# Turning V and K by VectorE and a DRAM scratch in the token mixer of a decoder layer, in place of TensorE transposes

## The chip, the cores and the metric

The kernel is one program on one core of a Trainium2 chip. Its time is device microseconds of one execution. The engines have a queue of instructions each and work through it in order: TensorE (PE; PEld are its weight loads), VectorE (DVE), ScalarE (ACT), GpSimd (POOL), and SyncE (SP), which here issues nearly all DMA transfers. An instruction whose data are not there stops its engine, and with it everything that stands behind it.

## The reference

One layer of a hybrid decoder for 280 tokens: 16 meta tokens and 256 prompt tokens (a sequence), and 8 tokens of 8 running requests. Model width 2048, all data fp32. The layer is FFN, mixer, FFN, each with a residual and a layer norm. What matters here is the mixer: one input projection makes ten parts, from which two branches follow.

```python
q_r, k_r, v_r, g_r, q_h, f_h, i_h, g_h, a_r, a_h = jnp.split(x @ w_in, N_PROJ, axis=-1)
# retention, 8 heads of 256, per chunk
o = jnp.einsum('bhij,bhjv->bhiv', inner, v) + jnp.einsum('bhid,bhdv->bhiv', q_dec, S)
S_new = jnp.exp(lg * C)[:, None, None].astype(S.dtype) * S + jnp.einsum('bhjd,bhjv->bhdv', k_dec, v)
# HGRN2, 16 heads of 128, per chunk
S_new = jnp.exp(b_last[:, :, 0, :, None]) * S + jnp.einsum('bhjd,bhjv->bhdv', k_dec, v)
```

A projection leaves its result with features on partitions and tokens along the free axis. The state updates contract over tokens (`j`), so `k_dec` and `v` must have tokens on partitions there, and the outputs need `v` in the same form. So V and K have to be turned once per head.

## The kernel before

Every large product is three fp32r matmuls: weights and tokens are split into a rounded part and a residue, and high x high, low x high, high x low are summed. Weights come in loads of eight 128x128 blocks, in the order in which they are used: `load` fetches `raw` (512 KB, SP queue, three buffers), ScalarE rounds it to `whi` (L188, three buffers), VectorE subtracts for `wlo` (L189, three buffers). So a load of `raw` can leave once the `wlo` three loads earlier is made, and `whi` of a load can be made once TensorE has used up the load three earlier. One load is 24 matmuls.

The mixer projects in groups of two column chunks (four loads a group). There are eight passes `u`, each one retention head and two HGRN2 heads: `qkv_groups(u)` in the order f, q_h, i_h, q_r, k_r, v_r, and the gate groups of the pass before. `evacuate` takes each result out of PSUM. Beside the projection run generators: after i_h `mix_hg(u)` is started, after v_r `mix_ret(u)`. `pump` is called after every k step of the projection and lets a generator go on when its count (the numbers after `yield`) is down. That is how the mixers' instructions come to stand between the projection's matmuls. TensorE's order is exactly the order written (`manual_schedule`); the order on ScalarE, VectorE, GpSimd and SP is set by the framework's scheduler when the program is built, and is fixed then.

Names of the change: `v` is a value part of the projection, `vth` and `vtr` the turned values of HGRN2 and retention, `kth` the turned HGRN2 K (one per head, `turned(h)`), `ks` and `vs` the split K and V of retention, `pst` (L1022, L1024) the HGRN2 state update, `psr` (L1168) the retention state update, `po` and `por` the outputs. `smh` and `vbh` are the running requests' states and values of an HGRN2 head; their loads for the second head are opened by small GpSimd copies that read `kth` (L769, L773), so they leave after it exists. `turned`, in the change, is a scratch in DRAM.

Turning is done by TensorE: `nc.tensor.transpose` of a 128x128 block into PSUM (L875 for i_h, L982 for K, L1107 for v_r, L1114 for k_r), and a ScalarE copy of two blocks out of it (L879, L983, L1108; for k_r the scaled split of L1129 and L1130 reads PSUM itself). That is sixteen transposes a pass.

## Time and profile before

| | us |
|---|---|
| three runs: median (lowest to highest) | 2566.79 (2566.35 to 2567.9) |
| profiled execution: span | 2563.9 |
| profiled execution: its own time | not recorded beside the span |
| TensorE busy | 2553.4 |
| VectorE busy | 1702.8 |
| ScalarE busy | 1392.2 |
| GpSimd busy | 57.0 |
| mean DMA rate, GB/s | 209 |

The median of the runs lies 2.9 us above the span of the profiled execution. The mixer lies between 745 and 1690 us of the span. In the profile's lists a row names the source line, the engine, the operation, what is written and read, and either (groups) the count, the busy time in us, the mean duration in ns and the idle time before, or (timelines) the start and the duration in us, merged over neighbours of one kind. The duration of a matmul holds its way through the array, so two matmuls in a row overlap in it; what one costs in a stream is the distance of the starts.

### The profile page before, as it was taken

The numbers are of one execution on the slowest core, as the hardware profiler recorded it, in microseconds if no ns is written. First come the engines' busy times: TensorE is split into PE (matmuls) and PEld (weight loads), VectorE is DVE, ScalarE is ACT, GpSimd is POOL, SyncE is SP. The second block draws the span as 40 slices with busy tenths as digits, with TensorE's granted clock in tenths as the row PEclk, the third lists the DMA queues.
The fourth block names the chain that finished last, engine by engine and source line by source line (L and its number), as shares of the span: only waits on it lengthen the run. The fifth ranks groups of instructions, "written<-read, shape, count | busy, mean of one in ns | idle before, by whom it ended". The sixth has DMA issues, their size and how long they took to land.

```text
span 2563.9 us, 56275 instructions
## 1 busy us (share of the span) xinstructions
PE 2553.4 (100%) x23424; PEld 2534.4 (99%) x23424; DVE 1702.8 (66%) x2827; ACT 1392.2 (54%) x2186; POOL 57.0 (2%) x152
## 2 busy tenths in 40 slices
PE   9999999999999999999999999999999999999999
PEld 9999999999999999999999999999999999999998
DVE  6444544475569878777777777777885555556555
ACT  5444444444456767767676666675564444444443
POOL 0000000000000000000000000000000000000000
PEclk9999999999999999999999999999999999999999
DMA  7555555555555876767676767675556565565554
GB/s 244 183 187 183 187 182 184 186 182 186 184 201 180 287 265 232 264 214 260 212 264 215 259 223 255 224 239 188 196 190 197 194 197 195 194 196 195 195 195 149
DMA packets 156897, 536.26 MB, mean 209 GB/s; under 512 B 17952, under 2 KB 25952, under 8 KB 156640
## 3 DMA queue, kind: packets, MB, share of 16 engines
q1 hardware_dynamic: 156352, 532.37, 62.0%
q8 instruction: 183, 3.00, 0.5%
q14 instruction: 74, 0.61, 0.1%
q10 hardware_dynamic: 288, 0.29, 0.0%
HBM read 501.99 MB, written 30.61 MB: 208 GB/s over the span
## 4 chain that ended last, share of the span: by engine, by line
PE 96%; DVE 2%; ACT 0%; issue 0%; DMA 0%; SPq 0%; ACTq 0%; DVEq 0%
PE up L218 36%; PE dn L218 19%; PE pj_i_h L218 3%; PE pj_g_r L218 3%; PE pj_q_h L218 3%; PE pj_g_h L218 3%; PE pj_a_r L218 3%; PE pj_a_h L218 3%; PE pj_f L218 3%; PE pj_q_r L218 3%; PE pj_k_r L218 3%; PE wo L218 3%; PE pj_v_r L218 3%; DVE wlo L189 1%; PE pqr L1211 1%; PE psr L1168 0%
## 5 line engine op out<-in xcount | busy, mean ns | idle before, releaser
L189 DVE TENSOR_TENSOR wlo<-raw,whi 128x1024 fp32r<-128x1024 f32 (+1 forms) x869 | 1062.2, 1223 | 740.7 <-ACT whi L188 737.3
L188 ACT CAST whi<-raw 128x1024 fp32r<-128x1024 f32 (+1 forms) x870 | 905.7, 1042 | 909.2 <-PE up L218 411.0
L218 PE MATMUL up<-xh,whi 128*128 128x280 f32 (+1 forms) x2624 | 725.6, 280 | 0.6 <-ACT whi L188 0.6
L218 PE MATMUL up<-xh,wlo 128*128 128x280 f32 (+1 forms) x2624 | 725.8, 280 | 0.4 <-DVE wlo L189 0.3
L218 PE MATMUL up<-xl,whi 128*128 128x280 f32 (+1 forms) x2624 | 725.4, 279 | 0.0
L218 PEld LDWEIGHTS up<-xh,wlo 128*128 128x128 f32 x2624 | 492.6, 189 | 1.0 <-DVE wlo L189 1.0
L218 PEld LDWEIGHTS up<-xh,whi 128*128 128x128 f32 x2624 | 492.6, 189 | 0.8 <-ACT whi L188 0.8
L218 PEld LDWEIGHTS up<-xl,whi 128*128 128x128 f32 x2624 | 492.6, 189 | 0.0
L218 PE MATMUL dn<-hh,whi 128*128 128x280 f32 (+1 forms) x1376 | 384.7, 280 | 0.0
L218 PE MATMUL dn<-hh,wlo 128*128 128x280 f32 (+1 forms) x1376 | 384.3, 279 | 0.0
L218 PE MATMUL dn<-hl,whi 128*128 128x280 f32 (+1 forms) x1376 | 384.3, 279 | 0.0
L218 PEld LDWEIGHTS dn<-hh,whi 128*128 128x128 f32 x1376 | 260.1, 189 | 0.1
L218 PEld LDWEIGHTS dn<-hl,whi 128*128 128x128 f32 x1376 | 260.1, 189 | 0.1
L218 PEld LDWEIGHTS dn<-hh,wlo 128*128 128x128 f32 x1376 | 260.1, 189 | 0.0
L218 PE MATMUL pj_k_r<-xh,whi 128*128 128x280 f32 x256 | 74.2, 290 | 0.0
L218 PE MATMUL pj_g_r<-xh,whi 128*128 128x264 f32 x256 | 74.0, 289 | 0.0
L218 PE MATMUL pj_v_r<-xh,whi 128*128 128x280 f32 x256 | 73.8, 288 | 0.0
L218 PE MATMUL pj_v_r<-xh,wlo 128*128 128x280 f32 x256 | 72.4, 283 | 0.3 <-DVE wlo L189 0.3
L218 PE MATMUL pj_g_h<-xh,whi 128*128 128x264 f32 x256 | 72.7, 284 | 0.0
L218 PE MATMUL pj_k_r<-xh,wlo 128*128 128x280 f32 x256 | 72.4, 283 | 0.0
L218 PE MATMUL pj_v_r<-xl,whi 128*128 128x280 f32 x256 | 72.3, 283 | 0.0
L218 PE MATMUL pj_k_r<-xl,whi 128*128 128x280 f32 x256 | 72.3, 283 | 0.0
(421 smaller groups left out, 5263.4 us busy)
## 6 DMA issues: line engine op xcount, KB each, us to landing
raw<-in_w_up SPq DMA_DIRECT2D x343, 512.0 KB, 4.1
raw<-in_w_in SPq DMA_DIRECT2D x320, 512.0 KB, 4.3
raw<-in_w_dn SPq DMA_DIRECT2D x172, 512.0 KB, 3.5
smr<-in_sr SPq DMA_DIRECT2D x32, 512.0 KB, 5.0
out_srs<-smr SPq DMA_DIRECT2D x32, 512.0 KB, 6.7
raw<-in_w_out SPq DMA_DIRECT2D x32, 512.0 KB, 3.9
vbr<-vrd SPq DMA_DIRECT2D x32, 256.0 KB, 4.1
smh<-in_sg SPq DMA_DIRECT2D x16, 512.0 KB, 5.2
```

Of the source, the lines that this page charges most:

```text
L188: nc.scalar.copy(hi[:, j:jn, :], raw[:, j:jn, :])
L189: nc.vector.tensor_tensor(out=lo[:, j0:j1, :], in0=raw[:, j0:j1, :], in1=hi[:, j0:j1, :].bitcast(F32), op=ALU.subtract)
L218: nc.tensor.matmul(o, w, t, start=start, stop=stop)
L1211: nc.tensor.matmul(pq[32 * j : 32 * j + 32, :256], qdr_at[c][:, 32 * b : 32 * b + 32], sms[2 * e + c][:, j, :], start=e + c == 0, stop=e + ...
```

## The change

V of both branches, K of HGRN2 and K of retention are no longer turned by TensorE. VectorE transposes every 32x32 block of a 128x256 tile within itself (`nc.vector.transpose`, straight out of PSUM for the values), writing the blocks so that four DMA transfers put them at their mirrored places in a DRAM scratch and a fifth reads the whole tile back in rows (`turned_over`). That is five calls a pass (i_h, two K, k_r, v_r) and 25 transfers, all on SP. The turned tiles have the layout (token in block, feature, chunk, block), so TensorE and the other engines read them with a stride of two or four elements. `ks` and the values' split read the turned tiles from SBUF; `v` serves as the staging tile for three of the calls, `k` for K. The ends and tails of the tokens that do not fill a block of 128 are still transposed by TensorE; ScalarE copies them out of PSUM now, where GpSimd took them from `v`.

```diff
@@ evacuate
                 elif n == "i_h":
...
+                    ends = tmp("ends", (P, 2, 2, NMETA))
+                    vt = tmp("vth", TURNED)
+                    v = tmp("v", TURNED)
+                    for j, o in enumerate(st.pop("i_h", (o0, o1))):
+                        nc.vector.transpose(pieces(v, j), o[:, NMETA:LP])
+                        nc.scalar.copy(ends[:, j, 0, :], o[:, :NMETA])
+                        nc.scalar.copy(ends[:, j, 1, :], o[:, T - NMETA : T])
+                    turned_over(vt, v)
...
+                    if n == "k_r":
+                        st["ks"] = ks = tmp("ks", (P, 2, *TURNED[1:]), dt=F32R, bufs=4, tag="smr")
+                        z = tmp("v", TURNED)
+                        for j in range(2):
+                            nc.vector.transpose(pieces(z, j), r[:, j, : 2 * P])
+                        turned_over(ks[:, 1].bitcast(F32), z)
...
                 elif n == "v_r":
-                    v = tmp("v", (P, 2, T))
-                    nc.scalar.copy(v[:, 0, :], o0)
-                    nc.scalar.copy(v[:, 1, :], o1)
-                    start(mix_ret(c0 // 2, st["q_r"], st["k_r"], v), 24 if c0 == 2 else 3)
+                    vt = tmp("vtr", TURNED)
+                    v = tmp("v", TURNED)
+                    for j, o in enumerate((o0, o1)):
+                        nc.vector.transpose(pieces(v, j), o[:, : 2 * P])
+                        nc.scalar.copy(tails[:, 2 + j, : T - 2 * P], o[:, 2 * P :])
+                    turned_over(vt, v)
+                    start(mix_ret(c0 // 2, st["q_r"], st["k_r"], st["ks"], vt), 24 if c0 == 2 else 3)
...
+            TURNED = (P, P, 2, 2)
...
+            def pieces(z, c):
+
+                return z[:, :, c].rearrange("p (i f) b -> p b i f", i=4)
+
+            def turned_over(out, z):
+
+                n = math.prod(z.shape[1:]) // 4
+                y = drp.tile([4, 32, 4, n], F32, tag=f"turned{n}", name="turned")
+                for i in range(4):
+                    nc.sync.dma_start(
+                        y[:, :, i, :].rearrange("j t r -> t j r"),
+                        z[32 * i : 32 * i + 32].rearrange("t (j f) c b -> t j (f c b)", j=4))
+                nc.sync.dma_start(out.rearrange("t f c b -> t (f c b)"), y.rearrange("j t i r -> (j t) (i r)"))
...
@@ mix_hg
                 for h in range(2):
 
-                    pt = mx_bank("pt")
-                    for b in range(2):
-                        nc.tensor.transpose(pt[:, b * P : (b + 1) * P], v[:, h, NMETA + b * P : NMETA + (b + 1) * P], ident)
...
                 def turned(h):
-                    kt = tmp("kth", (P, 2, P), bufs=2)
+                    kt = tmp("kth", (P, P, 1, 2), bufs=2)
                     kts.append(kt)
-                    pt = mx_bank("ptk")
-                    for b in range(2):
-                        t0 = NMETA + b * P
-                        nc.tensor.transpose(pt[:, b * P : (b + 1) * P], K[:, h, t0 : t0 + P], ident)
-                    nc.scalar.copy(kt, pt[:, : 2 * P].rearrange("p (b f) -> p b f", b=2))
+                    z = k[:, h, : 2 * P].rearrange("p (f c b) -> p f c b", c=1, b=2)
+                    nc.vector.transpose(pieces(z, 0), K[:, h, NMETA:])
+                    turned_over(kt, z)
...
-                        nc.tensor.matmul(pst[:, (b + 1) * P : (b + 2) * P], kts[h][:, b, :], vt[:, h, b, :], start=True, stop=True)
+                        nc.tensor.matmul(pst[:, (b + 1) * P : (b + 2) * P], kts[h][:, :, 0, b], vt[:, :, h, b], start=True, stop=True)
...
@@ mix_ret
                 for c in range(2):
-                    pt = mx_bank("pt")
+                    f = slice(c * P, (c + 1) * P)
                     for b in range(2):
-                        nc.tensor.transpose(pt[:, b * P : (b + 1) * P], v[:, c, b * P : (b + 1) * P], ident)
-                    nc.scalar.copy(vt[:, :, c, :], pt[:, : 2 * P].rearrange("p (b f) -> p b f", b=2))
-                    f = slice(c * P, (c + 1) * P)
-                    split(vs[:, 0, :, f], vs[:, 1, :, f], vt[:, :, c, :])
+                        split(vs[:, 0, b, f], vs[:, 1, b, f], vt[:, :, c, b])
                     yield 1
-                    pt = mx_bank("pt")
-                    for b in range(2):
-                        nc.tensor.transpose(pt[:, b * P : (b + 1) * P], k[:, c, b * P : (b + 1) * P], ident)
...
-                    todo = [(pt[:, b * P : (b + 1) * P], dec[:, b, u : u + 1], [ks[:, 0, b, f]], 0, ks[:, 1, b, f]) for b in range(2)]
+                    todo = [(ks[:, 1, :, c, b].bitcast(F32), dec[:, b, u : u + 1], [ks[:, 0, :, c, b]], 0, ks[:, 1, :, c, b]) for b in range(2)]
```

How the built program's instructions stand, in the fourth pass, at the places that the prediction speaks of. `raw127` to `raw136` are weight loads of the projection, counted from its start, and the same ones before and after; the numbers behind them only tell tiles apart.

SP's queue around the second turned K, before (the K was turned by TensorE, so nothing of it stands here; `vbh` and `smh` belong to the running requests):

```order
L770 DMA smh_14569<-in_sg 128x1024
L185 DMA raw128_14820<-in_w_in 128x1024
L774 DMA vbh_14570<-vh1d_14244 128x1024
L185 DMA raw129_14886<-in_w_in 128x1024
L185 DMA raw130_14929<-in_w_in 128x1024
L185 DMA raw131_14972<-in_w_in 128x1024
L1002 DMA out_sgs<-smh_14501 128x1024
L185 DMA raw132_15037<-in_w_in 128x1024
```

And now:

```order
L748 DMA turned_14655<-k_13953 32x4x64
L793 DMA smh_14619<-in_sg 128x1024
L185 DMA raw130_14989<-in_w_in 128x1024
L748 DMA turned_14655<-k_13953 32x4x64
L185 DMA raw131_15032<-in_w_in 128x1024
L748 DMA turned_14655<-k_13953 32x4x64
L748 DMA turned_14688<-v_14685 32x4x128
L185 DMA raw132_15097<-in_w_in 128x1024
L751 DMA kth_14653<-turned_14655 128x256
L748 DMA turned_14688<-v_14685 32x4x128 x3
L797 DMA vbh_14620<-vh1d_14291 128x1024
```

The writes of the block-turned K stand between the weight loads, the read back of `kth` behind raw132, and the load of `vbh`, which stood behind raw128, behind that read. On TensorE the place where this `kth` is used is the same as before, in the middle of the weights of raw127:

```order
L218 MATMUL pj_v_r7_14695<-xh1_13_9288,wlo127_14832 128x280
L1037 MATMUL pst_14849<-vm_8639,km_8638 128x128
L1039 MATMUL pst_14849<-vth_14209,kth_14611 128x128 x2
L1037 MATMUL pst_14858<-vm_8639,km_8638 128x128
L1039 MATMUL pst_14858<-vth_14209,kth_14653 128x128 x2
L218 MATMUL pj_v_r6_14694<-xh1_14_9292,whi127_14831 128x280
```

VectorE now has the updates that read this `vbh` ahead of the split of raw130, behind the block transposes of v_r:

```order
L694 STREAM_TRANSPOSE v_14879<-pj_v_r6_14694 128x2x128
L694 STREAM_TRANSPOSE v_14879<-pj_v_r7_14695 128x2x128
L1014 SCALAR_TENSOR_TENSOR smh_14619<-vbh_14620,meta_8644,smh_14619 128x128 x3
L189 TENSOR_TENSOR wlo130_14991<-raw130_14989,whi130_14990 128x8x128
L1014 SCALAR_TENSOR_TENSOR smh_14619<-vbh_14620,meta_8644,smh_14619 128x128 x5
```

SP's queue around the turned values of retention, now (before, this stretch of loads held only transfers of the running requests):

```order
L185 DMA raw134_15203<-in_w_in 128x1024
L748 DMA turned_14884<-v_14879 32x4x128
L185 DMA raw135_15233<-in_w_in 128x1024
L748 DMA turned_14884<-v_14879 32x4x128 x2
L1110 DMA smr_14917<-in_sr 128x1024
L185 DMA raw136_15275<-in_w_in 128x1024
L751 DMA vtr_14878<-turned_14884 128x512
```

The writes go out one by one behind raw133, raw134 and raw135, and the read behind raw136. ScalarE's split of these values stands behind the rounding of raw133 (before, its two halves stood behind raw130's and raw131's), and TensorE's `psr`, which uses `vs`, a quarter into the weights of raw131, as before:

```order
L188 CAST whi133_15162<-raw133_15161 128x8x128
L225 CAST vs_14916<-vtr_14878 128x128 x4
L1179 COPY sro_15052<-psr_15044 128x256
L1201 ACTIVATE smr_14917<-smr_14917,gam_15055 128x1024
L1201 ACTIVATE smr_14919<-smr_14919,gam_15055 128x1024
```

The passes after it have the same order; the first two differ in where the reads of `vtr` stand.

## The prediction

> **What bounds the kernel now.** I read the page's totals first, then its chain of work, then the list of who waited for whom on TensorE.

> ```profile
> span 2563.9 us, 56275 instructions
> PE 2553.4 (100%) x23424; PEld 2534.4 (99%) x23424; DVE 1702.8 (66%) x2827; ACT 1392.2 (54%) x2186; POOL 57.0 (2%) x152
> ...
> PE 96%; DVE 2%; ACT 0%; issue 0%; DMA 0%; SPq 0%; ACTq 0%; DVEq 0%
> ```
> ```profile
> PE pw L515 <- DVE eps_h L163: 1.0, 1, 1.0
> PE pt L1116 <- POOL tails L1103: 0.9, 1, 0.9
> ```

> TensorE is busy for 2553.4 of 2563.9 us and its longest wait is 1.0 us. So a matmul taken away is worth its full step, and a wait put into TensorE's stream costs its full length. Span and median differ by 2.9 us (2566.79 - 2563.9); I carry that over unchanged.

> **What is removed.** The four groups of transposes, and TensorE's timeline around one pair of them:

> ```profile
> L1107 PE MATMUL pt<-ident,v 128*128 128x128 f32 x32 | 6.2, 276 | 0.0
> L982 PE MATMUL ptk<-ident,K 128*128 128x128 f32 x32 | 6.1, 273 | 0.0
> L1114 PE MATMUL pt<-ident,k_r 128*128 128x128 f32 x32 | 6.1, 273 | 0.0
> L875 PE MATMUL pt<-ident,v 128*128 128x128 f32 x32 | 6.1, 273 | 0.0
> ```
> ```profile
> 1159.53 0.28 PE L218 MATMUL pj_a_r<-xh,wlo 128*128 128x264 f32 x1
> 1159.64 0.38 PE L1107 MATMUL pt<-ident,v 128*128 128x128 f32 x2
> 1159.78 0.36 PE L218 MATMUL pj_g_r<-xh,whi 128*128 128x264 f32 x1
> 1159.98 0.28 PE L218 MATMUL pj_g_r<-xl,whi 128*128 128x264 f32 x1
> 1160.09 0.28 PE L218 MATMUL pj_g_r<-xh,wlo 128*128 128x264 f32 x1
> ```

> The next plain matmul after 1159.98 starts at 1160.09: the step is 0.11 us. From 1159.53 to 1159.98 are four steps, 0.45 us, where two plain ones would be 0.22: the pair costs 0.23, 0.11 each. All 128 go (the transposes of ends and tails stay): **-14.1 us**.

> **What moves to engines with room.** The rows are a VectorE operation, a ScalarE evacuation, and the mixer's busy times (after the stretch and its length: TensorE, weight loads, VectorE, ScalarE, GpSimd, granted clock, DMA share, GB/s).

> ```profile
> 1138.42 0.42 DVE L240 TENSOR_TENSOR K<-K,T 128x256 f32<-128x256 f32 x1
> ```
> ```profile
> L1108 ACT COPY vtr<-pt x16: 362/372/384, 818.8 to 1668.8; 128x256 f32<-128x256 f32 x16
> ```
> ```profile
> 745.00:1690.00 945.00, 942.89 (x9533) 928.90 (x9532) 766.78 (x1561) 649.60 (x1235) 55.45 (x123) 1.00 0.71 240
> ```

> VectorE gets 64 block transposes of 128x256. No row shows one; at the 0.42 us of the nearest operation of that size they are 27 us. ScalarE loses 48 evacuations of 0.37 and the copies that made v, and gains small ones. TensorE is busy 942.89 of 945 us, VectorE 766.78, ScalarE 649.60: that work hides under TensorE, and I cost it at nothing; uncovered, it would be those 27 us. The same for bytes: each pass writes and reads back 1 MB, 16 MB in all beside 227 MB (240 GB/s over 945 us). SP issues 25 transfers more per pass, 200 in all; at 0.33 us each (its row below) that is 66 us of a queue that mostly waits for a free weight buffer, so nothing by itself. What they stand behind, and what stands behind them, is the matter.

> The strided reads of the turned tiles sit in 288 weight loads of TensorE (L1024, L1050, L1168, L1226). No row has a strided weight load. If each took one more step of 0.11 us that is 32 us; below, nothing. I take 0, because token operands that are read in two interleaved halves run at the plain step, and keep 32 for the range. [...]

> **What is added: a round trip behind the weight loads.** In the order, the second read back of a turned K (kth) stands on SP behind load raw132, and TensorE uses it in the middle of the weights of raw127. A load goes out only when the wlo three loads earlier is done. The fourth pass, in the timelines of TensorE, ScalarE, VectorE and SP:

> ```profile
> 1155.69 0.66 PE L1024 MATMUL pst<-vth,kth 128*128 128x128 f32 x4
> ```
> ```profile
> 1153.65 1.26 ACT L998 ACTIVATE smh<-smh,meta 128x128 f32<-128x128 f32 x4
> 1154.82 1.03 ACT L188 CAST whi<-raw 128x1024 fp32r<-128x1024 f32 x1
> ```
> ```profile
> 1155.88 1.23 DVE L189 TENSOR_TENSOR wlo<-raw,whi 128x1024 fp32r<-128x1024 f32 x1
> 1157.02 0.87 DVE L999 SCALAR_TENSOR_TENSOR smh<-vbh,meta,smh 128x128 f32<-128x128 f32 x3
> ```
> ```profile
> 1157.14 0.33 SPq L185 DMA_DIRECT2D raw<-in_w_in  x1
> ```
> ```profile
> vbr<-vrd SPq DMA_DIRECT2D x32, 256.0 KB, 4.1
> smh<-in_sg SPq DMA_DIRECT2D x16, 512.0 KB, 5.2
> ...
> vbh<-vh0d SPq DMA_DIRECT2D x8, 512.0 KB, 6.6
> out_srp<-sro SPq DMA_DIRECT2D x16, 128.0 KB, 2.3
> ```

> raw132 leaves at 1157.14, when wlo129 ends, and an issue takes 0.33: the read cannot leave before 1157.47, already 1.8 us after TensorE wanted the data. No such read exists yet. The fastest landing of this size is 2.3, the nearest in kind (a read back from a scratch) 4.1. Plainly that gives a wait of 1157.47 + 4.1 - 1155.69 = 5.9.

> In this pass it starts later. GpSimd's copy that opens the second state's load (smh) now follows its two meta copies:

> ```profile
> 1148.86 1.39 POOL L990 COPY meta<-fk 128x16 f32<-128x16 f32 x2 [0.28 <-PE ptm L988]
> ```

> So the load leaves at 1150.5 and lands 5.2 later, 1155.7. Four scalings of that state (1.26) stand ahead of whi129, which starts at 1157.0 in place of 1154.82; raw132 follows at 1159.3, the read at 1159.6, landing at 1163.7. **First wait: 8.0 us** (bounds 4.1, with a landing of 2.3 and no such delay, to 9.1, with one of 5.2).

> Next late is vbh: GpSimd lets SP send it only when kth has landed, and VectorE needs it for three updates (0.87) that stand ahead of wlo130. It leaves at 1164.0, lands 6.6 later, 1170.6; wlo130 ends 0.87 + 1.23 later, 1172.7. TensorE, released at 1163.7, has 7.3 us of prepared work (four matmuls and half of raw127's, 1.9, then raw128's and raw129's, 24 steps of 0.11 each) and arrives at 1171.0. **Second wait: 1.7** (0, or as much again, 3.4).

> The third is the state update psr. Its vs casts need vtr, whose read stands on SP behind raw136, while TensorE uses vs in the first quarter of raw131:

> ```profile
> 1168.74 0.94 PE L1168 MATMUL psr<-vs,ks 128*128 128x256 f32 x7
> ```
> ```profile
> 1163.91 0.69 DVE L1081 TENSOR_REDUCE cen<-vtr 128x2 f32<-128x512 f32 x1
> 1164.61 0.35 DVE L1130 SCALAR_TENSOR_TENSOR ks<-pt,dec,ks 128x128 fp32r<-128x128 f32 x1
> ...
> 1170.10 1.21 DVE L189 TENSOR_TENSOR wlo<-raw,whi 128x1024 fp32r<-128x1024 f32 x1
> ```
> ```profile
> 1171.33 0.33 SPq L185 DMA_DIRECT2D raw<-in_w_in  x1
> ```

> raw136 leaves when wlo133 is done, at 1171.33, the read at 1171.66, landing at 1175.8. VectorE has the reduction (0.69) and four residues (0.35 each) behind it: 1177.9, against 1168.74. **Third wait: 9.1** (6.3 with a landing of 2.3 and three casts of 0.36 alone; 11.9 with one of 5.2 and the second wait's 1.7 carried on). ScalarE stands at the vs cast with whi134 queued behind it, but raw131 to raw133 are prepared, so nothing more is late.

> Passes three to eight have this order: 6 x (8.0 + 1.7 + 9.1) = 112.8. The first two have the plain first wait, 2 x 5.9 = 11.8. Their vs casts stand earlier; I take 2.6 us for pass one (a split of 1.03 + 1.23 and three residues of 0.35, less the quarter of a load, 0.7, that TensorE does meanwhile) and 0 for pass two. Waits: **127.2 us**.

> **Restarts at half rate.** The warm-up matmuls of the first microseconds, early and late:

> ```profile
> L515 PE MATMUL pw<-ones x15: 421/421/421, 1.4 to 4.4; 128*128 128x128 f32 x15
> ```
> ```profile
> L515 PE MATMUL pw<-ones x4: 275/275/275, 5.0 to 5.3; 128*128 128x128 f32 x4
> ```

> An idle TensorE starts with a step of 0.21 us (3.0 over 14) and reaches 0.11 (0.3 over 3) between 4.4 and 5.0, 3.4 to 4.0 us after its first matmul at 1.0, though the granted clock reads 1.00 throughout. A restart therefore loses half of some 3.7, 1.8 us. No wait here is long enough to show whether 8 us counts as idle: 0 to 1.8. I take 1.8, since this start is the only row of an idle engine, for the 14 long waits: **+25.2**. [...]

> Sum on the span: 2563.9 - 14.1 + 127.2 + 25.2 = 2702.2; plus 2.9, **2705 us**.

> **Rivals.**

> *Waits without cold restarts.* For it: the granted clock never left 1.00. Against: nor did it during the slow start. 2705 - 25 = 2680. Chance 0.2.

> *Short round trips.* If small transfers land in 2.3 us and GpSimd and vbh delay nothing: 6 x (4.1 + 6.3) + 2 x 4.1 = 70.6, warm: 2566.8 - 14.1 + 70.6 = 2623. For it: out_srp's row. Against: the reads follow 512 KB loads in the same queue. Up to 2650, chance 0.13.

> *Everything late.* First wait 9.1, second 3.4, third 11.9, in the first two passes 1157.47 + 5.2 - 1155.69 = 7.0, and the weight loads' 32: 6 x 24.4 + 2 x 7.0 + 2.6 + 25.2 + 32 - 14.1 = 206, 2773. From 2740 up, chance 0.17. For it: in the stretch from 1146 to 1176 VectorE is busy 26.03 of 30 us and ScalarE 24.13, so little catches up.

> ```profile
> 1146.00:1176.00 30.00, 30.00 (x260) 29.90 (x259) 26.03 (x57) 24.13 (x57) 4.13 (x7) 1.00 0.75 258
> ```

> *Faster.* One mechanism: both reads land before TensorE asks, only the 14.1 us remain, 2552.7. That needs the kth read out by 1153.4 (1155.69 - 2.3); it would decide if SP ran one load further ahead. Against it stands the order: the read waits for the split that ends at 1157.11. Chance 0.04, and 0.02 for a draw, where few passes wait.

> **How the numbers follow.** The forecast keeps 0.44: 2705. The range takes the low bound and the high case, 2623 to 2775; what lies outside is the faster case and delays that no row bounds. A measurement of this kernel tells 0.2%, about 5 us, from no change; faster has 0.04, same 0.02, slower 0.94.

> **What would show it.** TensorE's waits should name pst for kth (DMA) and psr for vs, 8 and 6 or 7 times, with SP's own list showing reads behind raw loads; 128 matmuls gone at 0.11; after each long wait a stretch of matmuls 0.2 us apart with PEclk still 1.00. It is wrong if TensorE's waits stay under some 20 us in all, or if they name a raw load or wlo first.

## The result and the profile after

The changed kernel takes 2726.55 us (median; 2723.72 to 2728.23) against 2566.57 (2566.04 to 2567.9) for the kernel before on the same chip: the ratio is 1.062, with a 95% interval of 1.0605 to 1.0635. The forecast was 2705, so the change is slower by a little more than predicted. Of the executions behind the experiments, one of the four of experiment 1 took 9550.89 us, though its clock reads 1.00; nothing on record explains it, and experiment 1's figures are those of the other three.

From the page of the changed kernel, its totals and its chain:

```profile
span 2725.2 us, 56386 instructions
PE 2599.9 (95%) x23296; PEld 2576.9 (95%) x23296; DVE 1745.1 (64%) x2907; ACT 1388.5 (51%) x2172; POOL 26.3 (1%) x128
...
PE 85%; DMA 7%; DVE 4%; ACT 3%; issue 1%; SPq 1%; POOL 0%; DVEq 0%; ACTq 0%; POOLq 0%
```

Two numbers carry the loss. TensorE's idle time (span less busy) went from 10.5 to 125.3 us: 114.8 more. And its busy time went from 2553.4 to 2599.9 us, although 128 matmuls fewer are in it: 46.5 more, and 60.6 more if the 14.1 us of the removed transposes are counted. Idle time is waits; busy time that grows with fewer instructions means slower instructions. The waits, in the list of who waited for whom on TensorE (us in total, times, longest):

```profile
PE psr L1177 <- ACT vs L225: 62.9, 7, 11.5
PE pst L1039 <- DMA kth<-turned: 49.0, 8, 8.0
PE pt L1125 <- ACT tails L695: 2.6, 1, 2.6
```

The first wait in the fourth pass, in its timeline:

```profile
1208.81 0.35 SPq L185 DMA_DIRECT2D raw<-in_w_in  x1
...
1209.27 0.37 SPq L751 DMA_DIRECT2D kth<-turned  x1
...
1212.85 0.58 PE L1039 MATMUL pst<-vth,kth 128*128 128x128 f32 x1 [5.95 <-DMA kth<-turned]
```

TensorE asked at 1206.90 (1212.85 - 5.95). The read back left 2.4 us later, right behind a weight load, and landed 3.6 us after it left. The third wait, 14 us on:

```profile
1229.17 0.35 SPq L185 DMA_DIRECT2D raw<-in_w_in  x1
1230.85 0.33 SPq L751 DMA_DIRECT2D vtr<-turned  x1
...
1236.63 1.37 ACT L225 CAST vs<-vtr 128x128 fp32r<-128x128 f32 x4 [9.04 <-DMA vtr<-turned]
...
1237.74 2.25 PE L1177 MATMUL psr<-vs,ks 128*128 128x256 f32 x7 [10.44 <-ACT vs L225]
```

TensorE asked at 1227.30, the read left at 1230.85 and landed 5.8 us later; the casts that the first psr needs took the last 1.1. These waits are where the prediction had put them. What it missed is a part of the slower instructions.

### The profile page after: what moved, and what is told of

Read it like the earlier page. It is cut to its first block, busy times and chain, and to the rows that moved or that the text cites. A ratio compares the mean times of both kernels' runs of the same rounds, so it can differ in the third digit from the quotient of the medians.

```text
span 2725.2 us, 56386 instructions
## 1 busy us (share of the span) xinstructions
PE 2599.9 (95%) x23296; PEld 2576.9 (95%) x23296; DVE 1745.1 (64%) x2907; ACT 1388.5 (51%) x2172; POOL 26.3 (1%) x128
## 4 chain that ended last, share of the span: by engine, by line
PE 85%; DMA 7%; DVE 4%; ACT 3%; issue 1%; SPq 1%; POOL 0%; DVEq 0%; ACTq 0%; POOLq 0%
PE up L218 35%; PE dn L218 18%; PE pj_i_h L218 3%; PE pj_q_h L218 3%; PE wo L218 3%; PE pj_q_r L218 3%; PE pj_g_h L218 3%; PE pj_a_h L218 3%; PE pj_k_r L218 3%; PE pj_f L218 3%; PE pj_g_r L218 2%; PE pj_a_r L218 2%; DVE wlo L189 2%; DMA vtr<-turned 1%; ACT whi L188 1%; DMA ks<-turned 1%
## 5 line engine op out<-in xcount | busy, mean ns | idle before, releaser
L189 DVE TENSOR_TENSOR wlo<-raw,whi 128x1024 fp32r<-128x1024 f32 (+1 forms) x869 | 1062.1, 1222 | 747.9 <-ACT whi L188 743.9
L188 ACT CAST whi<-raw 128x1024 fp32r<-128x1024 f32 (+1 forms) x870 | 905.7, 1041 | 935.9 <-PE up L218 413.5
L218 PE MATMUL up<-xh,wlo 128*128 128x280 f32 (+1 forms) x2624 | 726.3, 280 | 0.4 <-DVE wlo L189 0.3
L218 PE MATMUL up<-xh,whi 128*128 128x280 f32 (+1 forms) x2624 | 726.0, 280 | 0.1
L218 PE MATMUL up<-xl,whi 128*128 128x280 f32 (+1 forms) x2624 | 725.8, 280 | 0.0
L218 PEld LDWEIGHTS up<-xh,wlo 128*128 128x128 f32 x2624 | 493.4, 189 | 1.0 <-DVE wlo L189 1.0
L218 PEld LDWEIGHTS up<-xh,whi 128*128 128x128 f32 x2624 | 493.4, 189 | 0.3 <-ACT whi L188 0.3
L218 PEld LDWEIGHTS up<-xl,whi 128*128 128x128 f32 x2624 | 493.4, 189 | 0.0
L218 PE MATMUL dn<-hh,whi 128*128 128x280 f32 (+1 forms) x1376 | 384.9, 280 | 0.0
L218 PE MATMUL dn<-hh,wlo 128*128 128x280 f32 (+1 forms) x1376 | 384.5, 279 | 0.0
L218 PE MATMUL dn<-hl,whi 128*128 128x280 f32 (+1 forms) x1376 | 384.5, 279 | 0.0
L218 PEld LDWEIGHTS dn<-hl,whi 128*128 128x128 f32 x1376 | 260.5, 189 | 0.1
L218 PEld LDWEIGHTS dn<-hh,whi 128*128 128x128 f32 x1376 | 260.4, 189 | 0.1
L218 PEld LDWEIGHTS dn<-hh,wlo 128*128 128x128 f32 x1376 | 260.5, 189 | 0.0
L1177 PE MATMUL psr<-vs,ks 128*128 128x256 f32 x112 | 30.7, 428 | 63.9 <-ACT vs L225 62.9
L1177 PEld LDWEIGHTS psr<-vs,ks 128*128 128x128 f32 x112 | 27.0, 318 | 66.6 <-ACT vs L225 64.3
L218 PE MATMUL pj_v_r<-xh,whi 128*128 128x280 f32 x256 | 77.7, 303 | 0.0
L218 PE MATMUL pj_v_r<-xh,wlo 128*128 128x280 f32 x256 | 76.2, 297 | 0.6 <-DVE wlo L189 0.6
L218 PE MATMUL pj_v_r<-xl,whi 128*128 128x280 f32 x256 | 76.0, 297 | 0.0
L218 PE MATMUL pj_g_r<-xh,whi 128*128 128x264 f32 x256 | 75.1, 294 | 0.0
L218 PE MATMUL pj_k_r<-xh,whi 128*128 128x280 f32 x256 | 74.3, 290 | 0.0
L218 PE MATMUL pj_k_r<-xh,wlo 128*128 128x280 f32 x256 | 73.4, 287 | 0.0
## 6 DMA issues: line engine op xcount, KB each, us to landing
raw<-in_w_up SPq DMA_DIRECT2D x343, 512.0 KB
raw<-in_w_in SPq DMA_DIRECT2D x320, 512.0 KB
raw<-in_w_dn SPq DMA_DIRECT2D x172, 512.0 KB
smr<-in_sr SPq DMA_DIRECT2D x32, 512.0 KB
out_srs<-smr SPq DMA_DIRECT2D x32, 512.0 KB
raw<-in_w_out SPq DMA_DIRECT2D x32, 512.0 KB
vbr<-vrd SPq DMA_DIRECT2D x32, 256.0 KB
smh<-in_sg SPq DMA_DIRECT2D x16, 512.0 KB
```

Of the source, the lines that this page charges most:

```text
L188: nc.scalar.copy(hi[:, j:jn, :], raw[:, j:jn, :])
L189: nc.vector.tensor_tensor(out=lo[:, j0:j1, :], in0=raw[:, j0:j1, :], in1=hi[:, j0:j1, :].bitcast(F32), op=ALU.subtract)
L218: nc.tensor.matmul(o, w, t, start=start, stop=stop)
L1177: nc.tensor.matmul(pairs(pst[:, :256]), kk, vv.rearrange("p c f -> p f c"), start=i == 0, stop=i == 6)
```

## The experiments

### 1. The interleaved tiles alone

```diff
-kt = tmp("kth", (P, 2, P), bufs=2)
+kt = tmp("kth", (P, P, 1, 2), bufs=2)
-nc.scalar.copy(kt, pt[:, : 2 * P].rearrange("p (b f) -> p b f", b=2))
+nc.scalar.copy(kt[:, :, 0, :].rearrange("p f b -> p b f"), pt[:, : 2 * P].rearrange("p (b f) -> p b f", b=2))
```

vth, vtr and ks go the same way; the kernel before is otherwise as it was.

> The kernel before, with its transposes on TensorE and no scratch; only the evacuations of K, the values and the retention keys write the interleaved layout that the change uses (keys and values of 128 tokens lie 8 or 16 bytes apart), so that the same 288 weight loads read with a stride. Theory A (a strided weight load costs a step of its own): in the trace of the change the four groups step by about 0.23 us in place of 0.11 even far from any wait, so pst +6.7, po +7.7, psr +11.4 and por +4.2, 30 us in all: 2596. Theory B (those steps were long only because TensorE had just stood idle or because transfers were in flight): no change, 2567.

Measured: 2599.49 us (three executions), ratio 1.0128 (1.0112 to 1.0145), 32.6 us above the kernel before, with no wait over 1.0 us on TensorE; its busy time is 2586.5, 33.1 more. Theory A holds. Two of its groups, weight load and matmul each (count, then min/median/max in ns), with the same of the kernel before behind them. This kernel:

```profile
L1050 PEld LDWEIGHTS po<-acch,vth x64: 307/320/333, 888.7 to 1747.5; 128*128 128x128 f32 x64
L1050 PE MATMUL po<-acch,vth x64: 384/395/399, 888.8 to 1747.6; 128*128 128x128 f32 x64
L1024 PEld LDWEIGHTS pst<-vth,kth x64: 195/213/217, 876.7 to 1691.5; 128*128 128x128 f32 x64
L1024 PE MATMUL pst<-vth,kth x64: 405/410/431, 876.8 to 1691.8; 128*128 128x128 f32 x64
```

The kernel before:

```profile
L1050 PEld LDWEIGHTS po<-acch,vth x64: 189/191/192, 884.8 to 1713.9; 128*128 128x128 f32 x64
L1050 PE MATMUL po<-acch,vth x64: 272/275/275, 884.9 to 1714.0; 128*128 128x128 f32 x64
L1024 PEld LDWEIGHTS pst<-vth,kth x64: 189/192/192, 873.8 to 1661.3; 128*128 128x128 f32 x64
L1024 PE MATMUL pst<-vth,kth x64: 275/275/325, 873.8 to 1661.4; 128*128 128x128 f32 x64
```

In vth the features of one operand lie 16 bytes apart in each partition, in kth 8. A weight load at 16 bytes takes 320 ns in place of 191, one at 8 bytes 213. In po the moving operand (acch) is plain, and the matmul grows with its load. In pst the load (kth, 8 bytes) takes only 21 ns longer; that the matmul still grows from 275 to 410 is put down to its moving operand (vth, 16 bytes), though no run changes one of the two alone. The distances from one start to the next, added up over each group, grew by 7.7 us in po, 11.7 in psr, 6.4 in pst and 4.3 in por: 30.0 of the 33. In po, psr and pst the median step is 0.23 us in place of 0.11.

### 2. Matmuls in the waits

```diff
 nc.tensor.matmul(pst[:, 0:P], km[:, h, :], vm[:, h, :], start=True, stop=True)
+for _ in range(20 * h):
+    nc.tensor.matmul(pst[:, 3 * P :], ones, ones, start=True, stop=True)
...
+for _ in range(38 if u > 1 and c == 0 else 0):
+    nc.tensor.matmul(pst[:, 2 * P : 3 * P], ones, ones, start=True, stop=True)
```

First with 40 and 80:

> The changed kernel, with matmuls of ones (never read) put into TensorE's order in front of the two waits: 40 before each second pst, 80 before the first psr of passes three to eight, so that TensorE works through most of the time that it would stand still. The waits' ends stay where they were. Theory A (the restarts after a wait are slow, because TensorE was idle): the steps of 0.2 us after these 14 waits go, 1.4 to 2.7 us each, some 25 us in all: 2701. Theory B (the slow steps come from something else, such as strided weights or transfers in flight): 2727, or more where the added matmuls outlast a wait.

Measured: 2783.89 us, ratio 1.0848. The fill was twice as long as meant (two instructions for each call) and outlasted both waits, so its time tests nothing; but behind these fills the weight matmuls step by 0.11 to 0.12 us from the second on, with no slow stretch. With half the number:

> The changed kernel, with matmuls of ones (never read) ahead of the two waits, now 20 and 38 of them: the run with 40 and 80 showed that each is two instructions of 0.112 us, so that the fill of 9 and 18 us outlasted the waits. 20 take 4.5 us of waits of 5 to 8, 38 take 8.5 of waits of 9 to 11.5. Theory A (restarts after an idle TensorE are slow): in the changed kernel the steps after these 14 waits lose 25 us against the plain ones, and go: 2701. Theory B (the slow steps have another cause): 2727.

Measured: 2720.19 us, ratio 1.0598 (1.058 to 1.0615), only 6 below the changed kernel. Its waits on TensorE:

```profile
PE psr L1181 <- ACT vs L225: 17.4, 7, 3.4
PE pst L1041 <- DMA kth<-turned: 11.8, 8, 2.7
```

The steps that begin while the granted clock is 0.50 exceed their groups' means at full clock by 28 us in all in the changed kernel and by 9 here. So the slow restarts are real and TensorE's idling makes them, but taking away 19 us of them gained 6. Where the restart behind pst is fast, TensorE reaches psr 12.8 us after it in place of 13.9 to 15.3, and waits there longer (with the added matmuls 11.0 us on average in passes three to eight, in place of 10.1): the values come when the queue brings them. Theory A was right on the cause and wrong on the worth.

### 3. One of the two late tensors back on TensorE

```diff
-nc.vector.transpose(pieces(z, 0), K[:, h, NMETA:])
-turned_over(kt, z)
+for b in range(2):
+    nc.tensor.transpose(pt[:, b * P : (b + 1) * P], K[:, h, t0 : t0 + P], ident)
+nc.scalar.copy(kt[:, :, 0, :].rearrange("p f b -> p b f"), ...)
```

> The changed kernel, with K of HGRN2 turned by TensorE again (32 transposes back, their evacuation writes the same interleaved tile), values and retention keys through the scratch as changed. Theory A (each wait stands for itself): the eight waits of pst go, 49 us, with their slow restarts, some 17, and the transposes come back, 3.5: 2664. Theory B (the wait moves on: psr then waits longer by what pst waited less, since its values come no earlier): 2700 or more. The first wait of the forecast was 8.0 in passes three to eight.

Measured: 2671.75 us, ratio 1.041 (1.0395 to 1.0426): 55 us back of the 62 that A expected. pst no longer waits; psr waits longer, 72.5 us in place of 62.9:

```profile
PE psr L1179 <- ACT vs L225: 72.5, 7, 11.9
```

The same with the retention values:

> The changed kernel, with the retention values turned by TensorE again (32 transposes back, evacuated into the same interleaved tile). Theory A: psr's waits go, 63.9 us, with their restarts and that of the tails, some 13, and the transposes come back, 3.5: 2653. pst's waits stay near 6 us. Theory B (TensorE only runs into the next late thing on the queue, such as the turned keys, whose read back stands just ahead): 2690 or more.

Measured: 2671.26 us, ratio 1.0408 (1.0392 to 1.0423): again 55, of 73. pst's waits are as they were, and smaller waits came up (psr for vs 6.9 us in 12 waits, the transposes for v 3.4 in the first pass):

```profile
PE pst L1040 <- DMA kth<-turned: 48.6, 8, 7.8
```

Both are mostly theory A: taking away the round trip of K or that of the retention values gives back about 55 us. Of what A expected beyond that, 7 and 18 us, a part goes to what is late next.

### 4. Plain tiles, round trips as they are

```diff
-turned_over(kt, z)
+turned_over(z, z)
+nc.scalar.copy(kt, z.rearrange("p f c b -> p (c b) f"))
```

vth likewise; the residues of the keys and the centring of the values write plain tiles.

> The changed kernel, but with the turned tiles put into plain order before TensorE loads them: ScalarE copies HGRN2's values and K after the read back, the residues of the retention keys and the centring of the retention values write plain tiles. No weight load is strided; the round trips stay on SP. Theory A (strides cost 33 us beside the waits, as in the kernel with interleaved tiles alone): 2694, and up to 4 us more since the copy of K (0.4 us) lies behind its read. Theory B (while TensorE waits anyway, the strides only fill time that the waits would take): 2715 or more.

Measured: 2720.13 us, ratio 1.0595 (1.058 to 1.0611): 6 us gained, where the strides alone cost 33. Theory B's side, and in part for its reason. po and por, far from the waits, are back at 7.1 and 9.3 us from 14.8 and 13.6. psr and pst give back only 6.6 us of some 17: in the changed kernel 64 of psr's 112 matmuls and 32 of pst's 64 run just behind a wait, at granted clock 0.50, and there a plain step takes 0.21 us, hardly less than the strided 0.23 to 0.24. The rest of the gain is taken by a third wait in each pass, for tails:

```profile
PE pst L1039 <- ACT kth L998: 47.9, 8, 6.8
PE psr L1179 <- ACT vs L225: 41.9, 7, 7.6
PE pt L1126 <- ACT tails L694: 19.5, 7, 3.4
```

The second copy of tails waits for VectorE, which in this kernel's order turns the second half of the retention values behind the updates that wait for vbh. The fourth pass, on VectorE and ScalarE:

```profile
1218.84 1.14 DVE L1014 SCALAR_TENSOR_TENSOR smh<-vbh,meta,smh 128x128 f32<-128x128 f32 x4 [1.37 <-DMA vbh<-vh1d]
...
1222.08 0.63 DVE L693 STREAM_TRANSPOSE vtr<-pj_v_r 128x256 f32<-128x256 f32 x1
```
```profile
1222.74 0.18 ACT L694 COPY tails<-pj_v_r 128x24 f32<-128x24 f32 x1 [1.52 <-DVE vtr L693]
```

psr's waits are 21 us shorter, those for tails 17 longer, and there are 21 waits of over 2 us in place of 16. The steps at half clock lose 44 us in place of 28 (counted as in experiment 2); that takes in the plain steps of psr and pst.

### 5. Another queue

```diff
-nc.sync.dma_start(
+nc.gpsimd.dma_start(
```

in all five transfers of a round trip.

> The changed kernel, with the five transfers of the round trip sent from GpSimd's queue in place of SP's; all else as changed, strided weight loads too. Theory A (the round trips are late because they stand behind weight loads on SP): the retention values' transposes end at 1217.6 in the fourth pass; four issues, a landing of 2.3, a read back of 3.5 to 5.8 and casts of 1.4 end at 1227 to 1229, and TensorE asks at 1227.3; kth's read leaves ten microseconds earlier. Both waits go but for 0 to 2 us, with their restarts: 2727 - 112 - 26 = 2589, up to 2605. Theory B (the transfers themselves are slow, or GpSimd, which waits for each group of transposes in order, passes the delay on): 2650 or more.

Measured: 2712.65 us, ratio 1.0566 (1.0549 to 1.0583). The queue does what A says for K: pst's waits fall from 49.0 to 1.8 us. But TensorE waits as long for something else:

```profile
PE pt L1125 <- ACT tails L695: 78.7, 7, 13.2
```

The fourth pass shows the chain, on ScalarE and GpSimd:

```profile
1203.91 0.35 POOL L1005 COPY meta<-fk 128x16 f32<-128x16 f32 x2
1209.81 0.57 POOL L751 DMA_DIRECT2D ks<-turned  x1 [5.55 <-DMA turned<-v]
```
```profile
1204.16 2.15 ACT L1013 ACTIVATE smh<-smh,meta 128x128 f32<-128x128 f32 x7 [4.33 <-POOL meta L1005]
...
1215.34 0.93 ACT L1138 ACTIVATE ks<-ks,dec 128x128 fp32r<-128x128 f32 x2 [4.99 <-DMA ks<-turned]
1216.17 1.03 ACT L188 CAST whi<-raw 128x1024 fp32r<-128x1024 f32 x1
...
1219.03 0.18 ACT L695 COPY tails<-pj_v_r 128x24 f32<-128x24 f32 x1 [0.98 <-DVE v L694]
```

GpSimd stands at the landings of a round trip's writes before it sends the read (116.5 us in 28 waits in all), the small copies (meta) queue behind, and the retention keys' read goes out only at 1209.81. ScalarE stands 4.99 us for it, with a weight cast behind; VectorE's split of that weight, its transposes and tails follow. This is theory B's second half. A read itself takes 2.4 to 6.7 us to land (median 4.1).

With plain tiles as well:

> Both edits together: round trips from GpSimd's queue, and plain tiles for the weight loads. Theory A (nothing but the waits, their restarts and the strides stood against the change): the 14.1 us of the transposes are left over, less what the first pass still waits: 2553 to 2565, against 2567 before. Theory B (as above for GpSimd's queue): 2620 or more.

Measured: 2719.8 us, ratio 1.0593 (1.0577 to 1.0609). Theory A is far off: the waits are spread over tails (30.7 us), km (21.7) and vs (21.2), and the clock falls to 0.50 in 20 stretches in place of 16.

### 6. Later uses

```diff
-yield 4 if u == 0 else 5
+yield 4 + 9 if u == 0 else 5 + 9
...
-yield 4
+yield 4 + (12 if u > 1 else 0)
```

> The changed kernel with its transfers on SP and its strided loads as they are; only TensorE's order differs: pst stands 9 steps of the weight stream later (all passes but the second), psr 12 steps later in passes three to eight, and what follows them is moved up by as much. Theory A (TensorE waits because the turned data come a fixed time after they are made, so a later use removes the waits): of the 118 us some 20 stay in the first passes, and the restarts go with the rest: 2600 to 2610. Theory B (the round trips pace the pass: ScalarE, VectorE and SP stand in their orders behind late data, so the weight stream itself comes late, and TensorE then waits for whi, wlo or tails): 2680 or more.

Measured: 2705.35 us, ratio 1.0541 (1.0525 to 1.0557): theory B. From pass three on pst and psr wait no more, and tails takes their place. TensorE's list, and the timeline of the fourth pass:

```profile
PE pt L1125 <- ACT tails L695: 83.6, 7, 14.2
```
```profile
1206.33 0.34 SPq L751 DMA_DIRECT2D kth<-turned  x1
...
1209.43 0.19 POOL L796 COPY vbh<-kth 128x1 f32<-128x1 f32 x1 [11.53 <-DMA kth<-turned]
1209.65 0.32 SPq L797 DMA_DIRECT2D vbh<-vh1d  x1
...
1216.90 2.19 DVE L1014 SCALAR_TENSOR_TENSOR smh<-vbh,meta,smh 128x128 f32<-128x128 f32 x8 [7.86 <-DMA vbh<-vh1d]
1219.12 1.08 DVE L694 STREAM_TRANSPOSE v<-pj_v_r 128x256 f32<-128x256 f32 x2
...
1219.78 0.18 ACT L695 COPY tails<-pj_v_r 128x24 f32<-128x24 f32 x1 [12.00 <-DVE v L694]
...
1220.56 0.45 PE L1125 MATMUL pt<-ident,tails 128*128 128x128 f32 x1 [13.74 <-ACT tails L695]
```

kth lands, GpSimd opens vbh, vbh lands 7 us later, VectorE updates, and only then turns the retention values, with tails behind. One edit more frees vbh from kth:

```diff
-nc.gpsimd.tensor_copy(vbs[h][:, 0, :1], kts[1][:, 0, 0, :1] if h else acc[:, 2 * P + 15 : 2 * P + 16])
+nc.gpsimd.tensor_copy(vbs[h][:, 0, :1], acc[:, 2 * P + 15 : 2 * P + 16])
```

> The run with the later uses, and one edit more: GpSimd's copy that opens the load of the second state's sample values (vbh) reads acch, which is ready early, and no longer kth, which comes from the scratch. In that run VectorE stands 7.9 us at the sample updates for vbh, with the transposes of the retention values queued behind them and tails behind those; TensorE then waits 13 to 14 us for tails in each of passes three to eight. Theory A (that chain kth, vbh, updates, transposes, tails sets the wait): vbh leaves some 8 us earlier and the waits for tails fall to 5 us or less: 2640 to 2660. Theory B (something else on SP or ScalarE is late by as much): 2690 or more.

Measured: 2686.47 us, ratio 1.0463 (1.0447 to 1.0479), 19 us better and still short of A: TensorE's waits for tails fall only from 83.6 to 69.2 us. vbh is in time; the transposes now stand for something else, in VectorE's list of waits:

```profile
DVE v L694 <- DMA turned<-v: 29.9, 6, 5.9
```

The tile v is single, and the scratch writes of the retention keys, each behind a weight load on SP, still read it. So this remedy, too, uncovers a transfer that stands behind weight loads. A second tile v was not tried.

### 7. Only what has room

Values of HGRN2 and retention keys through the scratch into plain tiles, K and the retention values on TensorE:

> Only the two round trips with room: HGRN2's values (used some 35 us after they are made) and the retention keys (made at 1196, used at 1227 in the fourth pass) go through the scratch on SP's queue and are put into plain tiles by ScalarE's copy and by the residues; K and the retention values are turned by TensorE as before. 64 transposes of 0.11 us go. Theory A (a round trip costs nothing where its use is far enough behind): 2566.8 - 7.0 = 2559.8, and no new wait over 1 us on TensorE. Theory B (a late read makes ScalarE stand in its order and delays the weight casts behind it, so that TensorE waits for tails or for whi, as in the run with GpSimd's queue): 2575 or more.

Measured: 2570.99 us, ratio 1.0018 (1.0009 to 1.0027). Neither theory's number: K's and the retention values' waits, restarts and strides are gone, but so is the gain. Idle time is 20.2 us against 10.5, with 3.4 us in the first pass and up to 0.8 in most later ones:

```profile
PE pj_g_r L218 <- DVE wlo L189: 3.5, 7, 0.8
```

With HGRN2's values alone:

> The kernel before, with HGRN2's values alone through the scratch (VectorE's block transposes, SP's queue, one copy by ScalarE that puts them into a plain tile); K, the retention values and the retention keys on TensorE. 32 transposes go. The run with values and keys came out at 2571, 11 us over its 2560, with TensorE waiting 0.8 us per pass for wlo and 3.4 for v in the first. Theory A (a round trip whose use is 35 us away costs nothing; the 11 us came with the keys): 2566.8 - 3.5 = 2563.3. Theory B (any of these transfers on SP delays weight loads a little in each pass): 2567 or more.

Measured: 2569.99 us, ratio 1.0012 (1.0003 to 1.0021): theory B's number, though in the first pass alone. The waits of the later passes are gone, so they came with the keys; the first pass still waits (whi 1.1, wlo 1.0, v 2.0, tails 0.9). TensorE's idle time is 15.6 us, 5.1 more than before, and its busy time fell by 0.5 where the 32 transposes are 3.5. Of the missing 3.0, 1.5 are the steps of one stretch at half clock in the first pass; the rest is open. None of the kernels tried beats the kernel before.

## Why the prediction was right, and where it was not

**The sum.** The forecast added 138.3 us to the span, the chip 161.3. By terms:

| term | forecast | measured | from |
|---|---|---|---|
| transposes | -14.1 | -14.1 | 128 matmuls fewer; taken as forecast |
| waits | 127.2 | 114.8 | growth of TensorE's idle time |
| strided operands | 0 | 33.1 | experiment 1, busy time |
| slow restarts | 25.2 | 27.5 | what is left of the 60.6; 28 by their steps (experiment 2) |
| sum | 138.3 | 161.3 | |

So the result is near the forecast partly by luck: one term was too large and another missing. Among the waits, too, errors cancel: in all passes the first was forecast at 59.8 us and measured at 49.0, the second at 10.2 and did not come, the third at 57.2 and measured at 62.9. Between strides and restarts the split holds in this order alone, as the two hardly add up behind a wait (at clock 0.50 a plain step takes 0.21 us and a strided one 0.23 to 0.24, experiment 4).

**The strided reads** are the step that failed. "I take 0, because token operands that are read in two interleaved halves run at the plain step" took operands of another pattern (two plain halves read in turn, as in psr, which steps by 0.11 us in the kernel before) for elements that lie 16 bytes apart. Its bound, one more step of 0.11 us for each, was the right value: 32. In experiment 1 a weight load took 320 ns at 16 bytes and 213 at 8, against 191 in plain tiles. The prediction also looked at weight loads only; in pst the moving operand is strided as well.

**First wait.** Forecast 8.0 in passes three to eight; measured 5.5 to 6.5. The read left 2.4 us after TensorE asked, where 3.9 was forecast: the delay by GpSimd's order, put at 2.2, was small, as ScalarE stood 1.14 us for smh. The landing took 3.6, not 4.1. The plain 5.9 would have been right.

**Second wait.** Forecast 1.7 in six passes; it did not come. vbh landed 5.0 us after it left, not 6.6, and TensorE, at a granted clock of 0.50 for 4.25 us behind the first wait, came later. The chain itself is real: in experiment 6, with pst out of the way, it sets the pass.

**Third wait.** Forecast 9.1, measured 9.2 to 11.5. The read left 3.5 us after TensorE asked (2.9 forecast) and landed in 5.8, above the bound of 5.2, with 512 KB loads issued just ahead of it.

**Restarts.** Counted well (1.8 each against about 1.7), though "with PEclk still 1.00" was wrong. The 1.00 over the first microseconds was no reading: the clock record of the kernel before begins at 4.90 us, between the last slow step (to 4.83) and the first fast one (to 5.09). Busy times of TensorE, its weight loads, VectorE, ScalarE and GpSimd, then the granted clock, DMA share and GB/s, in the stretch of the first wait of the fourth pass, behind it, and 4 us later, and last behind the third wait:

```profile
1206.90:1212.85 5.95, 0.00 (x1) 0.00 (x0) 1.92 (x3) 2.07 (x6) 0.00 (x0) 0.78 0.67 212
1212.85:1217.10 4.25, 4.25 (x18) 4.25 (x19) 1.48 (x4) 0.59 (x2) 0.19 (x1) 0.50 0.46 182
1217.10:1221.10 4.00, 4.00 (x38) 4.00 (x37) 3.56 (x10) 2.11 (x5) 0.00 (x0) 1.00 0.53 191
...
1237.74:1241.00 3.26, 3.26 (x13) 3.07 (x14) 2.46 (x8) 0.93 (x3) 0.19 (x1) 0.51 0.51 160
```

The clock reads 0.50 and 0.51 for 4.25 and 3.26 us behind the waits.

**What was costed at nothing.** VectorE's block transposes took 0.43 us (K) and 0.65 to 0.67 (the others) in place of 0.42, 39 us in place of 27, but no wait of TensorE names them. That the queue's order was the matter is borne out, in a stronger form than predicted: the parts aren't independent, and experiments 2 to 6 gave back less than their term each time. The terms tell where the time was, not what an edit is worth.

## What to carry to other kernels

A round trip through DRAM on a queue that also carries waiting weight loads is priced by what stands ahead of it (in the fourth pass the two late reads left 2.4 and 3.5 us after TensorE asked) and by every engine that stands at its landing in its order (ScalarE 9.04 us for vtr). With the use some 35 us behind, the waits of the later passes were gone, and even then nothing was gained here (experiment 7). Removing one wait shows the next: without pst's, psr's grew from 62.9 to 72.5 us. Before matmul operands change their layout, look at the distance between the elements that one load reads: at 16 bytes the step of po and psr was 0.23 us in place of 0.11. A few microseconds saved on TensorE can be lost to one idle stretch and its restart: in experiment 7 the 3.5 us of the 32 transposes stood against 5.1 us more idle time and 1.5 at half clock.

## What was not expected of the hardware

The same idle time doesn't always cost a restart. Ahead of tails in the first pass TensorE is idle for 2.62 us in several of these kernels. In the run with K back on TensorE, the stretch before and behind it (columns as in the last view):

```profile
818.00:820.90 2.90, 0.28 (x4) 0.10 (x3) 2.84 (x6) 1.77 (x5) 0.00 (x0) 1.00 0.64 197
820.90:824.30 3.40, 3.40 (x85) 3.22 (x86) 3.20 (x6) 3.34 (x9) 0.00 (x0) 1.00 0.74 219
```

In the run with 20 and 38 matmuls in the waits:

```profile
818.00:820.90 2.90, 0.28 (x4) 0.10 (x3) 2.85 (x6) 1.77 (x5) 0.00 (x0) 0.89 0.64 192
820.90:824.30 3.40, 3.40 (x52) 3.26 (x56) 3.18 (x6) 3.34 (x9) 0.00 (x0) 0.59 0.75 204
```

85 matmuls at clock 1.00, or 52 at 0.59, behind the same wait. In the same run, an idle time of 1.40 us was followed by 1.74 us at a granted clock of 0.99 and only then by 3.36 at 0.50:

```profile
1207.70:1209.44 1.74, 1.74 (x10) 1.69 (x11) 0.24 (x1) 0.27 (x1) 0.19 (x1) 0.99 0.12 41
1209.44:1212.80 3.36, 3.36 (x17) 3.36 (x16) 2.58 (x5) 1.20 (x3) 0.00 (x0) 0.50 0.82 285
```

```profile
816.86:820.27 3.41, 1.41 (x12) 1.20 (x11) 3.02 (x7) 2.09 (x4) 0.00 (x0) 1.00 0.73 222
```
```profile
818.92:822.33 3.41, 1.44 (x12) 1.47 (x13) 3.35 (x7) 3.20 (x8) 0.00 (x0) 1.00 0.65 205
```

The first was followed by 0.50, the second by 1.00. A window at full clock in which TensorE was busy for less than 42% was followed by 0.50 in every case, one over 76% in none; in between, busy time alone doesn't decide (42% was followed by 1.00 above; in the changed kernel 54%, from 1056.65 us, by 0.50 and 63%, from 981.55 us, by 1.00), and what does stays open. No wholly idle window was needed: the 1.40 us of idle time above lay in a window that was 59% busy.
